# Head norms of a differential attention: given priority on VectorE, and head 7's spreading products one step later on TensorE

## The chip, the cores and the metric

The kernel runs on one core of a Trainium2 chip. The metric is the device time of one execution in microseconds; the time before is the median of three runs. Names of engines: PE is TensorE (PEld its weight loads), DVE is VectorE, ACT is ScalarE, SP is the engine that issues the DMAs.

## The reference

Two post-norm layers over 512 tokens of width 1024. In each layer three branches (a bidirectional state-space scan, a differential attention, a cross-attention to 256 memory tokens) work on projections of x; each branch's output is projected to 1024, weighted by a sigmoid gate, and the sum is projected once more. The change lies in the differential attention, of 8 heads:

```python
q = _apply_rope(dq.reshape(Bsz, S, DIFF_HEADS, 2, DIFF_HEAD_DIM), cos, sin)
k = _apply_rope(dk.reshape(Bsz, S, DIFF_HEADS, 2, DIFF_HEAD_DIM), cos, sin)
v = dv.reshape(Bsz, S, DIFF_HEADS, 2 * DIFF_HEAD_DIM)
o = _diff_attention(q, k, v, lam)          # (softmax_1 - lam * softmax_2) v, per head
o = _rmsnorm(o, diff_norm_w[layer]) * (1.0 - lambda_init)
y_diff = o.reshape(Bsz, S, DIFF_WIDTH) * jax.nn.silu(dg.astype(jnp.float32))
...
merged = (gates[:, :, 0] * jnp.einsum('bse,ed->bsd', y_ssd, w_br_ssd[layer])
          + gates[:, :, 1] * jnp.einsum('bse,ed->bsd', y_diff, w_br_diff[layer])
          + ...)
```

The norm of a head needs 1 / sqrt(mean(o^2) + eps) for each token: one number per token and head, by which 128 channels are multiplied.

## The kernel before, in words

All wide products are done in three passes of split fp32 numbers: a weight `wr` of 512 KB is fetched by SP (line 138), rounded to `wh` by ACT and reduced to the remainder `wl` by DVE (`split`), and each 128-column block is multiplied as wl by xh, wh by xl, wh by xh (`mm3`). The results stand in three PSUM banks `pj`. One such product for 512 tokens is a unit of 24 matmuls. `wr` has two buffers, `wh` and `wl` three each. The engines take their instructions in order. A scheduler sets the order of each, by priorities and estimated times; inside `manual_schedule` PE's own instructions keep the order in which they are written, though others may be put between them. `late(n)` lowers the priority of what is recorded under it by n; `late(-300)` raises it.

The attention of a layer (`diff`) is a list of 35 steps. Each step runs one unit of projection in two halves of 12 matmuls, and puts jobs of the attention before it (`first`) and between its halves (`amid`): `scores` of the next block of 128 queries, `turn` (the transposition of the weights of this one, through the single PSUM bank `pt`, then split into `wT`), `values` for two blocks, and `sums`, which adds up the squares of a head's output (`fth`, held in the tile `sq`) into `ss`. Attention has 32 blocks, steps 0 to 31 (`nst` is 32). The units of steps 28 to 34 are the gates 1 to 7 of this branch; so gate 6 is step 33 and gate 7 step 34.

`norm` (lines 919 to 929) computes the reciprocal norms: a reciprocal, a few products and a Newton iteration (`rsqrt`, tiles rs_q, rs_u, rs_y) in seventeen small instructions on DVE. For heads 0 to 6 `norms` does this in step 30 for 28 columns, transposes the result on PE into `pt` (line 111), copies it to `rt` (ACT), and writes it to DRAM as `rd`. `fin(h)` then reads one row of `rd` back, spread over 128 partitions, into a buffer `fth` (line 954; two buffers, which the squares use too), multiplies the head's output `sdy` with it on DVE, and splits the product into `dy` (rounded half on ACT, remainder on DVE). For head 7 `last` spreads the norms without DRAM: PE multiplies them, broadcast, with the identity into a bank `pm` (pm<-rs_y), and `fin(7)` multiplies with that bank. `last` stands between the halves of step 33.

Behind the steps come the eight branch outputs (`branch_out`): each is a unit of 24 matmuls pj<-dy over the eight heads in order, whose first needs the `dy` of head 0 and whose last that of head 7.

Of the kernel before, what the change touches and what calls it, by code (L numbers as in the profile page):

```python
# [15 lines left out]
ALU = mybir.AluOpType  # L16
# [4 lines left out]
P = 128  # L21
S = 512
D = 1024
KC = D // P
NL = 2
M = 256
EPS = 1e-5
# [14 lines left out]

LX, LD = 70, 80

FILL = (0, 2, 0, 2, 0, 4, 0, 0)

# [3 lines left out]
def bc(ap, shape):  # L52
    return ap.broadcast_to(shape)


class Net:
# [728 lines left out]
    def diff(self, l):  # L785
        nc = self.nc
# [131 lines left out]

        def norm(lo, hi):

            n = 4 * (hi - lo)
            s0, ss = self.s0[:, 4 * lo:4 * hi], self.ss[:, 4 * lo:4 * hi]
            nc.vector.reciprocal(out=s0, in_=s0)
            self.stt(ss, ss, 1.0 / 128.0, s0, ALU.mult, ALU.mult)
            self.tt(ss, ss, s0, ALU.mult)
            self.ts(ss, ss, EPS, ALU.add)
            r = self.rsqrt(self.fp, ss, n)
            self.tt(r, r, s0, ALU.mult)
            return r

        def norms():

            n = 4 * (KC - 1)
            r = norm(0, KC - 1)
            pt = self.bank(self.pt, "pt")
            self.tr(pt[:n, :P], r)
            rt = self.t(self.fp, [n, P], "rt", bufs=1)
            self.act(rt, pt[:n, :P])
            self.rd = self.t(self.dp, [n, P], "rd")
            nc.sync.dma_start(out=self.rd, in_=rt)  # L940

        def last():

            r = norm(KC - 1, KC)
            self.rb = self.bank(self.pm, "pm")
            for c in range(4):
                self.mm(self.rb[:, c * P:(c + 1) * P], bc(r[:, c:c + 1], [P, P]), self.ident)
# [12 lines left out]
        def step(unit, *parts):  # L960

            def f(wh, wl):
                g = fn(wh, wl)
                for p in parts:
                    for job in p:
                        job()
                    next(g, None)
            fn, u = unit
            self.T(f, u)

        def job(fn, *a):
            return lambda: fn(*a)
# [17 lines left out]
        nst = 4 * KC  # L990
        for s, unit in enumerate(units):
            first = [job(scores, s + 1)] if s + 1 < nst else []
            amid = []
            if s % 4 == 2 and s < nst:
                amid.append(job(values, s // 4, 0))
            if s % 4 == 0 and 0 < s <= nst:
                amid.append(job(values, s // 4 - 1, 1))
            if s < nst:
                amid.append(job(turn, s))
            if s % 4 == 1 and 1 < s <= nst + 1:  # L1000
                first.append(job(sums, s // 4 - 1))
            if s == nst - 2:
                amid.append(norms)
            if s == nst + 1:
                amid.append(last)
            step(unit, first, amid)
            if s >= nst - 1:
                for h in range(2 * (s - nst + 1), min(2 * (s - nst + 1) + 2, KC)):
                    self.T(job(fin, h))
        self.T(order.close)  # L1010
        mgs = ([], [])

# [216 lines left out]
```

## Time and profile before

| | us |
|---|---|
| median of 3 runs | 2241.68 (2237.81 to 2244.03) |
| the profiled execution, its own time | 2240.25 |
| its span | 2238.5 |
| PE busy | 2173.2 (97%) |
| DVE busy | 1589.9 (71%) |
| ACT busy | 1004.6 (45%) |
| mean granted PE clock | 0.994 |

The page gives busy times, the chain of work that ended last, and groups of instructions by line. The views of the trace give single instructions with start and length in us from the span's start (the timeline), who waited for whom, and busy times and clock in chosen stretches (windows). In brackets behind an instruction stands how long its engine had been idle before it and whose end released it. The two layers run the same code; attention ends at about 1025 us in the first and 2141 us in the second.

### The profile page before, as it was taken

How to read it: one execution, taken by the hardware profiler on the slowest of the kernel's cores; microseconds unless marked ns; L12 is line 12 of the kernel's file. 1: busy time of each engine (PE TensorE's matmuls, PEld its weight loads, DVE VectorE, ACT ScalarE, POOL GpSimd, SP SyncE). 2: the span in 40 equal slices, each digit the busy share in tenths (PEclk: the TensorE clock that was granted, in tenths of full speed). 3: DMA queues.
4: the chain of work that ended last, by engine and by line, in shares of the span. 5: the costliest groups of instructions: out<-in, count | busy, mean ns of one | idle time of the engine just before them, and what ended most of it. 6: DMA issues, size and time to landing. Idle time of an engine off the chain costs nothing.

```text
span 2238.5 us, 30344 instructions
## 1 busy us (share of the span) xinstructions
PE 2173.2 (97%) x11714; PEld 1787.8 (80%) x11714; DVE 1589.9 (71%) x2468; ACT 1004.6 (45%) x1895; POOL 52.9 (2%) x38
## 2 busy tenths in 40 slices
PE   8999999999999999998999999999999999999898
PEld 6777877788888788877996777787788887888678
DVE  7887888758544777765567888888744547777657
ACT  5664545424432555442355564554423325544430
POOL 0000000000000000000000000010100000000000
PEclk9999999999999999999999999999999999999999
DMA  4654444425453222233564545453433332223333
GB/s 148 180 160 144 147 142 138 126 85 190 145 179 115 90 81 82 81 104 108 163 225 115 165 141 151 132 152 122 123 124 118 116 106 85 78 84 90 109 99 128
DMA packets 108278, 283.79 MB, mean 127 GB/s; under 512 B 12588, under 2 KB 17252, under 8 KB 107876
## 3 DMA queue, kind: packets, MB, share of 16 engines
q1 hardware_dynamic: 108132, 281.84, 41.2%
q8 instruction: 92, 1.51, 0.3%
q14 instruction: 54, 0.44, 0.1%
HBM read 255.55 MB, written 17.85 MB: 122 GB/s over the span
## 4 chain that ended last, share of the span: by engine, by line
PE 71%; DVE 14%; DMA 7%; ACT 5%; issue 2%; SPq 0%; POOL 0%; DVEq 0%; POOLq 0%; ACTq 0%
PE pj L103 59%; PE pm L103 9%; DMA ab<-dab 4%; DVE wl L81 2%; PE pt L111 2%; DVE ab L81 2%; DVE acc L84 2%; ACT ab L91 1%; ACT wh L91 1%; DVE y L81 1%; DVE rx L81 1%; PE pt L103 1%; DMA wr<-wu 1%; DMA fth<-rd 1%; DVE yl L84 1%
## 5 line engine op out<-in xcount | busy, mean ns | idle before, releaser
L103 PE MATMUL pj<-xh,wl 128*128 128x512 f32 x1664 | 669.1, 402 | 10.8 <-DVE wl L81 8.9
L103 PE MATMUL pj<-xh,wh 128*128 128x512 f32 x1664 | 660.8, 397 | 0.0
L103 PE MATMUL pj<-xl,wh 128*128 128x512 f32 x1664 | 658.1, 395 | 0.0
L81 DVE TENSOR_TENSOR wl<-wr,wh 128x1024 fp32r<-128x1024 f32 x330 | 404.5, 1226 | 108.3 <-ACT wh L91 107.5
L91 ACT ACTIVATE wh<-wr 128x1024 fp32r<-128x1024 f32 x330 | 347.4, 1053 | 235.3 <-PE pj L103 199.5
L103 PEld LDWEIGHTS pj<-xh,wl 128*128 128x128 f32 x1664 | 314.1, 189 | 90.8 <-issue 18.3
L103 PEld LDWEIGHTS pj<-xh,wh 128*128 128x128 f32 x1664 | 313.7, 189 | 71.6 <-issue 6.0
L103 PEld LDWEIGHTS pj<-xl,wh 128*128 128x128 f32 x1664 | 314.1, 189 | 63.5 <-issue 3.6
L91 ACT ACTIVATE ab<-ab,bias 128x128 f32<-128x128 f32 x512 | 160.7, 391 | 121.9 <-DVE ab L81 121.3
L84 DVE SCALAR_TENSOR_TENSOR acc<-pj,hcw,acc 128x510 f32<-128x510 f32 x192 | 142.4, 743 | 23.8 <-ACT acc L91 22.4
L91 ACT ACTIVATE fpp<-pm,fmx 128x512 f32<-128x512 f32 x128 | 87.9, 687 | 83.4 <-DVE fmx L881 82.6
L881 DVE TENSOR_REDUCE fmx<-pm 128x1 f32<-128x512 f32 x128 | 87.0, 686 | 45.4 <-PE pm L103 45.1
L103 PE MATMUL pj<-yl,wh 128*128 128x512 f32 x256 | 102.3, 400 | 0.8 <-DVE yl L84 0.8
L103 PE MATMUL pj<-yh,wh 128*128 128x512 f32 x256 | 103.1, 403 | 0.0
L81 DVE TENSOR_TENSOR ab<-ab,cst 128x1024 f32<-128x1024 f32 x64 | 86.3, 1349 | 22.9 <-DMA ab<-dab 22.8
L103 PE MATMUL pj<-dy,wh 128*128 128x512 f32 (+1 forms) x384 | 101.9, 354 | 0.0
L103 PE MATMUL pj<-yh,wl 128*128 128x512 f32 x256 | 101.9, 399 | 0.0
L103 PE MATMUL pj<-cy,wh 128*128 128x512 f32 x256 | 78.8, 389 | 0.0
L103 PEld LDWEIGHTS pj<-dy,wh 128*128 128x128 f32 x384 | 68.0, 189 | 10.0
L103 PE MATMUL pj<-wh,xl 128*128 128x256 f32 x256 | 74.8, 292 | 0.0
L103 PE MATMUL pj<-wl,xh 128*128 128x256 f32 x256 | 72.4, 283 | 0.0
L103 PE MATMUL pj<-wh,xh 128*128 128x256 f32 x256 | 72.3, 283 | 0.0
(273 smaller groups left out, 3387.3 us busy)
## 6 DMA issues: line engine op xcount, KB each, us to landing
wr<-wu SPq DMA_DIRECT2D x336, 512.0 KB, 3.6
ab<-dab SPq DMA_DIRECT2D x64, 512.0 KB, 5.7
eb<-deb SPq DMA_DIRECT2D x64, 256.0 KB, 4.8
mkv<-dkv SPq DMA_DIRECT2D x16, 512.0 KB, 4.3
rsw<-rx SPq DMA_DIRECT2D x128, 64.0 KB, 2.0
dgt<-tg SPq DMA_DIRECT2D x18, 256.0 KB, 2.6
dkv<-mo SPq DMA_DIRECT2D x16, 256.0 KB, 4.0
dkv<-q SPq DMA_DIRECT2D x16, 256.0 KB, 3.7
```

The costliest lines, as they stand in the source:

```text
L81: (eng or self.nc.vector).tensor_tensor(out=out, in0=a, in1=b, op=op)
L84: self.nc.vector.scalar_tensor_tensor(out=out, in0=a, scalar=s, in1=b, op0=op0, op1=op1)
L91: self.nc.scalar.activation(out=out, in_=a, func=f, **kw)
L103: self.nc.tensor.matmul(out=out, lhsT=a, rhs=b, start=first, stop=last)
L111: self.nc.tensor.transpose(out=out, in_=x, identity=self.ident)
L881: nc.vector.tensor_reduce(out=mx[:, c:c + 1], in_=ps, axis=AX.X, op=ALU.min)
```

## The change

`norm` is no longer called by the jobs that use its result. It is recorded by itself, behind step 29 (heads 0 to 6) and behind step 33 (head 7), with its priority on DVE raised by 300. `spread` (before: `norms`) transposes, copies and writes as before, in step 30. `last` moves from step 33 to step 34. The `fin` jobs follow later: heads 0 and 1 behind step 32 (before: 31), heads 2 to 4 behind step 33 (before: 2 and 3 behind 32, 4 and 5 behind 33), heads 5 to 7 behind step 34.

```diff
-LX, LD = 70, 80
+LX, LD, LN = 70, 80, 300
...
         def norm(lo, hi):
-            n = 4 * (hi - lo)
             s0, ss = self.s0[:, 4 * lo:4 * hi], self.ss[:, 4 * lo:4 * hi]
-            nc.vector.reciprocal(out=s0, in_=s0)
-            self.stt(ss, ss, 1.0 / 128.0, s0, ALU.mult, ALU.mult)
-            self.tt(ss, ss, s0, ALU.mult)
-            self.ts(ss, ss, EPS, ALU.add)
-            r = self.rsqrt(self.fp, ss, n)
-            self.tt(r, r, s0, ALU.mult)
-            return r
-
-        def norms():
+            with self.late(-LN):
+                nc.vector.reciprocal(out=s0, in_=s0)
+                self.stt(ss, ss, 1.0 / 128.0, s0, ALU.mult, ALU.mult)
+                self.tt(ss, ss, s0, ALU.mult)
+                self.ts(ss, ss, EPS, ALU.add)
+                self.r = self.rsqrt(self.fp, ss, 4 * (hi - lo))
+                self.tt(self.r, self.r, s0, ALU.mult)
+
+        def spread():
             n = 4 * (KC - 1)
-            r = norm(0, KC - 1)
             pt = self.bank(self.pt, "pt")
-            self.tr(pt[:n, :P], r)
+            self.tr(pt[:n, :P], self.r)
...
         def last():
-            r = norm(KC - 1, KC)
+            r = self.r
...
             if s == nst - 2:
-                amid.append(norms)
-            if s == nst + 1:
+                amid.append(spread)
+            if s == nst + 2:
                 amid.append(last)
             step(unit, first, amid)
-            if s >= nst - 1:
-                for h in range(2 * (s - nst + 1), min(2 * (s - nst + 1) + 2, KC)):
-                    self.T(job(fin, h))
+            if s in (nst - 3, nst + 1):
+                self.T(job(norm, *((0, KC - 1) if s < nst else (KC - 1, KC))))
+            for h in {nst: (0, 1), nst + 1: (2, 3, 4), nst + 2: (5, 6, 7)}.get(s, ()):
+                self.T(job(fin, h))
```

What this makes of the order of the instructions, in the first layer (the second is alike). First PE, from the sums of head 7's squares (pt<-fth) to the first branch output. Before, pj_8870 is gate 6, pj_8938 gate 7, pj_8982 branch output 0, and pm<-rs_y is `last`:

```order
L103 MATMUL pt_8864<-cst_81,fth_8831 128x1 x4
L103 MATMUL pj_8870<-xh_82,wl_8753 128x512
...
L103 MATMUL pm_8903<-cst_81,rs_y_8887 128x128 x4
L103 MATMUL pj_8870<-xh_82,wl_8753 128x512
...
L103 MATMUL pj_8938<-xh_82,wl_8803 128x512
...
L103 MATMUL pj_8982<-dy_1008_6051,wl_8861 128x512
```

In the changed kernel pj_8860 is gate 6, pj_8928 gate 7 and pj_8982 again branch output 0:

```order
L103 MATMUL pt_8854<-cst_81,fth_8821 128x1 x4
L103 MATMUL pj_8860<-xh_82,wl_8753 128x512
...
L103 MATMUL pj_8928<-xh_82,wl_8793 128x512
...
L103 MATMUL pj_8982<-dy_1008_6051,wl_8851 128x512
...
L103 MATMUL pm_8941<-cst_81,rs_y_8891 128x128 x4
L103 MATMUL pj_8928<-xh_82,wl_8793 128x512
...
L103 MATMUL pj_8982<-dy_1009_6052,wh_8850 128x512
```

`last` moved behind the second half of gate 6, the first half of gate 7 (12 matmuls each) and the first ten matmuls of branch output 0, which the scheduler put ahead of it: three for each of the heads 0 to 2 and one for head 3. The second half of gate 7 and the rest of branch output 0 stand behind it. The transposition of the other heads' norms stands where it stood, behind the turn of step 30.

Next DVE, at the end of head 7's norms. The names fth_ are the spread rows that `fin` reads (before: 8927 is head 5, 8965 head 6), wl_ the weights' remainders, dy1 the remainders of the heads, pm_8903 `last`. Before:

```order
L81 TENSOR_TENSOR sdy_1014_6064<-sdy_1014_6064,fth_1526_8927 128x512
L84 SCALAR_TENSOR_TENSOR rs_y_1520_8887<-rs_q_1522_8889,rs_y_1520_8887 128x4
L81 TENSOR_TENSOR rs_q_1522_8889<-rs_y_1520_8887 128x4
L81 TENSOR_TENSOR sdy_1014_6064<-sdy_1014_6064,fth_1532_8965 128x512
L81 TENSOR_TENSOR rs_q_1522_8889<-rs_q_1522_8889,rs_u_1521_8888 128x4
L81 TENSOR_TENSOR dy1_1009_6052<-sdy_1014_6064,dy0_1008_6051 128x512
L84 SCALAR_TENSOR_TENSOR rs_y_1520_8887<-rs_q_1522_8889,rs_y_1520_8887 128x4
L81 TENSOR_TENSOR dy1_1009_6052<-sdy_1014_6064,dy0_1008_6051 128x512
L81 TENSOR_TENSOR rs_y_1520_8887<-rs_y_1520_8887,fs0_1015_6065 128x4
L81 TENSOR_TENSOR sdy_1014_6064<-sdy_1014_6064,pm_1523_8903 128x512
```

In the changed kernel fth_8912 is head 3, 8917 head 4, 8960 head 5, and wl_8925 the weight of branch output 1:

```order
L81 TENSOR_TENSOR sdy_1014_6064<-sdy_1014_6064,fth_1523_8912 128x512
L81 TENSOR_TENSOR rs_q_1521_8893<-rs_y_1519_8891 128x4
L81 TENSOR_TENSOR wl_1527_8925<-wr_1525_8922,wh_1526_8924 128x1024
L81 TENSOR_TENSOR rs_q_1521_8893<-rs_q_1521_8893,rs_u_1520_8892 128x4
L81 TENSOR_TENSOR dy1_1009_6052<-sdy_1014_6064,dy0_1008_6051 128x512
L84 SCALAR_TENSOR_TENSOR rs_y_1519_8891<-rs_q_1521_8893,rs_y_1519_8891 128x4
L81 TENSOR_TENSOR sdy_1014_6064<-sdy_1014_6064,fth_1524_8917 128x512
L81 TENSOR_TENSOR rs_y_1519_8891<-rs_y_1519_8891,fs0_1015_6065 128x4
L81 TENSOR_TENSOR sdy_1014_6064<-sdy_1014_6064,fth_1531_8960 128x512
L81 TENSOR_TENSOR dy1_1009_6052<-sdy_1014_6064,dy0_1008_6051 128x512
L81 TENSOR_TENSOR sdy_1014_6064<-sdy_1014_6064,pm_1529_8941 128x512
```

The norms of head 7 now end between the products of heads 4 and 5, where they ended behind the product of head 6; the product of head 7 comes ahead of that of head 6.

Last SP's queue from the writing of `rd` on. Before:

```order
L940 DMA rd_1497_8734<-rt_1496_8732 28x128
L954 DMA fth_1505_8790<-rd_1497_8734 128x512
L954 DMA fth_1506_8795<-rd_1497_8734 128x512
L138 DMA wr_1515_8858<-wu 128x1024
L138 DMA wr_1527_8932<-wu 128x1024
L954 DMA fth_1513_8848<-rd_1497_8734 128x512
L954 DMA fth_1514_8853<-rd_1497_8734 128x512
L954 DMA fth_1525_8922<-rd_1497_8734 128x512
L138 DMA wr_1534_8976<-wu 128x1024
L954 DMA fth_1526_8927<-rd_1497_8734 128x512
L954 DMA fth_1532_8965<-rd_1497_8734 128x512
```

In the changed kernel:

```order
L938 DMA rd_1497_8734<-rt_1496_8732 28x128
L138 DMA wr_1513_8848<-wu 128x1024
L138 DMA wr_1525_8922<-wu 128x1024
L952 DMA fth_1511_8838<-rd_1497_8734 128x512
L952 DMA fth_1512_8843<-rd_1497_8734 128x512
L952 DMA fth_1522_8907<-rd_1497_8734 128x512
L138 DMA wr_1534_8976<-wu 128x1024
L952 DMA fth_1523_8912<-rd_1497_8734 128x512
L952 DMA fth_1524_8917<-rd_1497_8734 128x512
L952 DMA fth_1531_8960<-rd_1497_8734 128x512
L138 DMA wr_1540_9013<-wu 128x1024
L952 DMA fth_1532_8965<-rd_1497_8734 128x512
```

The reads for heads 0 and 1 moved behind two weight loads. Heads 0, 1, 2 take the places of heads 2, 3, 4, heads 3 and 4 those of 5 and 6, and the reads for heads 5 and 6 follow, the last behind one more weight load.

## The prediction

> **What bounds the kernel now.** I read the page's busy times and its chain first.
>
> ```profile
> PE 2173.2 (97%) x11714; PEld 1787.8 (80%) x11714; DVE 1589.9 (71%) x2468; ACT 1004.6 (45%) x1895; POOL 52.9 (2%) x38
> PE 71%; DVE 14%; DMA 7%; ACT 5%; issue 2%; SPq 0%; POOL 0%; DVEq 0%; POOLq 0%; ACTq 0%
> ```
>
> TensorE (PE) sets the end, so an edit is worth what it takes from PE's idle or slow time. The view of waits, for PE alone, in the stretch where attention ends, shows two waits in the first layer (the second layer's long one is in the timeline below). Columns: waiting and awaited group, total us, times, longest.
>
> ```profile
> PE pm L103 <- DVE rs_y L81: 8.2, 1, 8.2
> PE pt L111 <- DVE wT L81: 1.4, 1, 1.4
> ```
>
> The long one is `last`: the spreading products (pm<-rs_y) stand between the halves of gate 6 and wait for head 7's norms. The timeline of PE (start, length; 30 products from 1018.14 to 1024.95), first layer and second:
>
> ```profile
> 1005.44 0.39 PE L103 MATMUL pj<-xh,wh 128*128 128x512 f32 x1
> 1013.99 2.08 PE L103 MATMUL pm<-cst,rs_y 128*128 128x128 f32 x8 [8.16 <-DVE rs_y L81]
> 1018.14 0.39 PE L103 MATMUL pj<-xh,wl 128*128 128x512 f32 x1
> 1024.95 0.39 PE L103 MATMUL pj<-dy,wl 128*128 128x512 f32 x1
> 2121.04 0.39 PE L103 MATMUL pj<-xh,wh 128*128 128x512 f32 x1
> 2129.38 2.08 PE L103 MATMUL pm<-cst,rs_y 128*128 128x128 f32 x8 [7.96 <-DVE rs_y L81]
> 2140.74 0.39 PE L103 MATMUL pj<-dy,wl 128*128 128x512 f32 x1
> ```
>
> A product of 512 columns takes 6.81 / 30 = 0.227 us. PE could have gone on at 1005.44 + 0.23 = 1005.67, but started its first branch product (pj<-dy) at 1024.95: 19.28 us, for `last` and 36 products. What `last` costs when PE isn't cold stands in the branch before, where the same eight matmuls spread another norm:
>
> ```profile
> 455.42 1.13 PE L103 MATMUL pm<-cst,rs_y 128*128 128x128 f32 x8
> 456.31 0.48 PE L103 MATMUL pj<-yh,wh 128*128 128x512 f32 x1
> 456.62 0.40 PE L103 MATMUL pj<-yh,wl 128*128 128x512 f32 x1
> ```
>
> That is 0.89, and 0.08 more for the first product behind it: 0.97. So 0.97 + 36 x 0.227 = 9.14 us would do, and the wait costs 10.1 us in the first layer (10.3 in the second, from 2121.27 to 2140.74): 8.3 idle, and 1.8 (2.2) because PE comes back slow. The windows (PE, PEld, DVE, ACT, POOL busy, granted clock, DMA share, GB/s) show that:
>
> ```profile
> 1014.00:1018.50 4.50, 4.50 (x16) 3.98 (x17) 1.38 (x2) 0.63 (x1) 0.00 (x0) 0.58 0.00 0
> 1018.50:1025.00 6.50, 6.50 (x31) 5.37 (x30) 1.23 (x1) 1.64 (x2) 0.00 (x0) 1.00 0.21 56
> ```
>
> The clock is 0.58 just after the wait and 1.00 later. [...]
>
> From there to the layer's end the chain is PE alone (start, length), so what is won stays won:
>
> ```profile
> 1016.06 120.43 PE pj L103 x804
> 2131.46 97.78 PE pj L103 x612
> ```
>
> **The change part by part.** No instruction is added or removed; rows move.
>
> *The first seven heads' norms go ahead on DVE.* Their transposition does not move on PE. It waits today for its PSUM bank (wT evicts it), not for the norms:
>
> ```profile
> 976.13 0.75 DVE L84 SCALAR_TENSOR_TENSOR fpp<-fpp,fsm 128x512 f32<-128x512 f32 x1
> 979.22 0.19 DVE L81 TENSOR_TENSOR rs_y<-rs_y,fs 128x28 f32<-128x28 f32 x1
> 984.31 0.60 PE L111 MATMUL pt<-cst,fpp 128*128 128x128 f32 x4
> 986.32 0.28 PE L111 MATMUL pt<-cst,rs_y 128*28 128x128 f32 x1 [1.41 <-DVE wT L81]
> ```
>
> The norms were done at 979.4, 6.9 us before that. So this part gains nothing. It costs nothing either: fpp, which is pushed back by the small norm instructions (at most a dozen, 0.2 us each), has from 976.9 to 984.3. Without that cover it would be 2.4 us a layer.
>
> *`last` moves behind 24 gate products and 10 branch products on PE.* That is cover for the wait: 34 x 0.227 = 7.7 us, so PE reaches `last` at 1013.39 instead of 1005.67. What it then finds depends on two things, both worked out for the first layer by putting the new orders onto the times that the old slots show.
>
> *The heads' rows come later.* On SP's queue the first two reads fth<-rd, the row that spreads a head's norms, now stand behind two more weight loads. Heads 0, 1, 2 take the slots that heads 2, 3, 4 had. The queue's timeline, and the landing times of fth<-rd:
>
> ```profile
> 988.30 0.82 SPq L954 DMA_DIRECT2D fth<-rd  x2
> 998.62 0.42 SPq L954 DMA_DIRECT2D fth<-rd  x1
> 1003.03 0.80 SPq L954 DMA_DIRECT2D fth<-rd  x2
> 1007.16 0.99 SPq L954 DMA_DIRECT2D fth<-rd  x2
> DMA to landing us min/median/max: 3.1/3.7/3.9
> ```
>
> and DVE's products with them:
>
> ```profile
> 1002.32 0.69 DVE L81 TENSOR_TENSOR sdy<-sdy,fth 128x512 f32<-128x512 f32 x1 [1.46 <-DMA fth<-rd]
> 1003.88 1.23 DVE L81 TENSOR_TENSOR wl<-wr,wh 128x1024 fp32r<-128x1024 f32 x1 [0.87 <-ACT wh L91]
> 1006.44 0.69 DVE L81 TENSOR_TENSOR sdy<-sdy,fth 128x512 f32<-128x512 f32 x1 [0.74 <-DMA fth<-rd]
> 1007.12 0.69 DVE L81 TENSOR_TENSOR sdy<-sdy,fth 128x512 f32<-128x512 f32 x1
> 1009.51 0.16 DVE L81 TENSOR_TENSOR rs_q<-rs_y 128x4 f32<-128x4 f32 x1
> 1009.71 0.16 DVE L81 TENSOR_TENSOR rs_q<-rs_q,rs_u 128x4 f32<-128x4 f32 x1
> 1010.91 0.69 DVE L81 TENSOR_TENSOR sdy<-sdy,fth 128x512 f32<-128x512 f32 x1 [0.45 <-DMA fth<-rd]
> 1013.78 0.15 DVE L81 TENSOR_TENSOR rs_y<-rs_y,fs 128x4 f32<-128x4 f32 x1
> ```
>
> Heads 0 to 3 are multiplied at 1002.3, 1006.4, 1007.1 and 1010.9. There are two fth buffers, so head 4's row is read when head 2's product ends (1007.8), head 5's after head 3's (1011.6), head 6's after head 4's.
>
> *Head 7's norms.* In DVE's new order head 3's product (1010.91 to 1011.6) is followed by a weight remainder wl (1.23, to 1012.8), head 3's remainder dy (0.69, to 1013.5) and head 4's product (to 1014.2) before the last rs_y: 1014.25. That is 0.3 us later than its 1013.93 now. So "ahead on DVE" doesn't bring head 7's norms forward; they still hang on the landings that DVE waits for in between. PE has the ten branch products' data in time (heads 0 to 2 are split by 1009.4; head 3's first half, on ACT, by 1012.3, and is wanted at 1013.16). PE waits 0.9 us at `last`. A gap of 1.4 us, the transposition's, shows what such a gap does to the clock:
>
> ```profile
> 986.68 0.39 PE L103 MATMUL pj<-xl,wh 128*128 128x512 f32 x1
> 986.91 0.40 PE L103 MATMUL pj<-xh,wh 128*128 128x512 f32 x1
> ```
>
> The pitch behind it is 0.23 at once, so I count no slow clock.
> *The rest of branch output 0.* A head's halves take (min/median/max, ns)
>
> ```profile
> L91 ACT ACTIVATE dy<-sdy x16: 617/630/631, 993.0 to 2132.2; 128x512 fp32r<-128x512 f32 x16
> L81 DVE TENSOR_TENSOR dy<-sdy,dy x16: 681/686/693, 994.0 to 2132.9; 128x512 fp32r<-128x512 f32 x16
> ```
>
> `last` ends at 1014.31 + 0.97 = 1015.28, gate 7's second half at 1018.00, eight products for heads 3 to 5 at 1019.8. Head 5's row lands at 1011.65 + 3.7 = 1015.35; head 6's is issued at 1014.25 and lands at 1017.95. DVE does head 5's product (to 1016.0), head 4's remainder (1016.65), head 7's product (1017.25), the remainders of 5 and 7 (1018.65), head 6's product (1019.3). ACT then halves head 6 (0.63, to 1020.0, behind gate 7's tanh), DVE takes its remainder by 1020.7. PE wants that at 1020.05: 0.9 us of waiting in all from 1019.8. With five products more, branch output 0 is done at 1021.9. Today it is done at 1024.95 + 24 x 0.227 = 1030.4.
>
> **Sum.** First layer 8.5 us. In the second layer the slots lie 1115.6 us later almost exactly (2121.27 against 1005.67), and its old excess is 0.2 larger: 8.7. Together 17.2. The profiled execution took 2240.25 us with a span of 2238.5, so its successor would have a span of 2221.3 and take 2223.1; against the median of the runs, 2241.68, which is 1.4 above it, 2224.5. That is the forecast. A measurement of this kernel can tell about 0.3%, 6.7 us, from no change.
>
> Bounds: at best PE waits for nothing, 10.1 + 10.3 = 20.4 us, 2221.3. At worst for the same mechanism the landings are all 3.9 and each step on DVE or ACT that I packed tightly slips a little, 2 us a layer: 2228.5.
>
> **Rivals.**
>
> *Head 7's norms come so late that the clock drops again.* By the rows the gap that does it lies between 1.4 us (it didn't) and 8.0 (it did); I take 4, nearer to the first, as an estimate. Then rs_y slips by 3.1 us. For it: DVE works in order, and three awaited things (a row, a weight, a row) stand ahead of rs_y. Against: each has a slot in the trace, with at most 1.5 us of waiting. Price: 3.1 + 2.0 for the clock, less the 0.9 at head 6 that it then covers: 4.2 a layer, 2232.9. [...]
>
> *Everything hides* (head 6's row and rs_y a microsecond earlier each): 2221.3.
>
> *Slower: the two fth buffers become the bound.* Branch products now stand ahead of `last` and of half of gate 7, and their data starts ten microseconds later (998.62 against 988.30). One buffer carries heads 0, 2, 4, 6 in turn, four trips. The gain is gone when head 6 is 8.5 us later than I have it: 2.1 us a trip, a landing of 5.8 instead of 3.7. At 7.0 it is 13.2 - 8.5 = 4.7 us lost a layer: 2251. The slowest row of the kind is
>
> ```profile
> ab<-dab SPq DMA_DIRECT2D x64, 512.0 KB, 5.7
> ```
>
> with twice the bytes, and the fth rows lie between 3.1 and 3.9 with weight loads beside them. So it is unlikely.
>
> *Nothing moves*: since rs_y isn't done earlier than today, the wait could simply stay if PE's new rows waited for their data as long as PE waited for rs_y. With a landing of 5.7 that is so: 4 x 2.0 = 8 of the 8.5, 2240.7.
>
> **How the numbers follow.** Forecast 0.78; all hidden 0.08; clock drop 0.08; nothing 0.04; slower 0.02. The forecast, all hidden and the drop are faster by over 0.3%: 0.94. The range goes from 2219 (all hidden, 2 us for the scatter of the runs, 2237.8 to 2244.0) to 2233 (the clock drop).
>
> **What would show it.** In the profile after: PE's wait at `last` under 2 us, with DVE's rs_y ending about where it did; PE's branch products beginning before `last`, at about 1011.1; a short wait of dy before the end of branch output 0; the granted clock near 1.00 through 1005 to 1025; fth<-rd first issued at about 998.6, still landing in 3 to 4 us. I am wrong if the wait turns up at pj<-dy for several microseconds, if rs_y ends after 1016, or if the clock still falls.

## The result, and the profile after

| | before | after |
|---|---|---|
| median of the runs (us) | 2242.53 (6 runs, 2237.81 to 2244.36) | 2222.06 (6 runs, 2220.18 to 2229.46) |
| the profiled execution (us) | 2240.25 | 2229.46 |
| its span (us) | 2238.5 | 2227.7 |
| mean granted PE clock | 0.994 | 0.995 |

The ratio is 0.9914, with an interval of 0.9897 to 0.993: the change takes 20.5 us by the medians, and between 16 and 23 by the interval. The profiled execution happens to be the longest of the six; the other five lie between 2220.18 and 2222.32. What made it long stands in the last section.

The page's busy times and chain hardly differ from those before, since no instruction was added or removed:

```profile
PE 2176.8 (98%) x11714; PEld 1789.9 (80%) x11714; DVE 1588.1 (71%) x2468; ACT 1004.9 (45%) x1895; POOL 53.9 (2%) x38
PE 70%; DVE 14%; DMA 8%; ACT 6%; issue 2%; SPq 0%; POOL 0%; POOLq 0%; DVEq 0%; ACTq 0%
```

The change shows in the waits. PE's own, at the end of attention in the first layer and then in the second:

```profile
PE pt L111 <- DVE wT L81: 1.4, 1, 1.4
PE pm L103 <- DVE rs_y L81: 0.7, 1, 0.7
...
PE pm L103 <- DVE rs_y L81: 1.3, 1, 1.3
```

The wait at `last` fell from 8.2 and 8.0 us to 0.7 and 1.3. The transposition's wait of 1.4 stayed, as its place did.

The timeline of PE in both layers: the sums of head 7 (pt<-cst,fth), the first branch product, `last`, and in the first layer the first product behind `last` (1016.47), the last two of head 6 (1021.51) and the first product of branch output 1 (1022.77):

```profile
1003.30 0.95 PE L103 MATMUL pt<-cst,fth 128*128 128x1 f32 x8
1012.40 0.39 PE L103 MATMUL pj<-dy,wl 128*128 128x512 f32 x1
1015.56 1.16 PE L103 MATMUL pm<-cst,rs_y 128*128 128x128 f32 x8 [0.73 <-DVE rs_y L81]
1016.47 0.48 PE L103 MATMUL pj<-xh,wl 128*128 128x512 f32 x1
1021.51 0.73 PE L103 MATMUL pj<-dy,wh 128*128 128x512 f32 x2
1022.77 0.39 PE L103 MATMUL pj<-dy,wl 128*128 128x512 f32 x1
2115.33 0.95 PE L103 MATMUL pt<-cst,fth 128*128 128x1 f32 x8
2124.43 0.39 PE L103 MATMUL pj<-dy,wl 128*128 128x512 f32 x1
2128.14 1.16 PE L103 MATMUL pm<-cst,rs_y 128*128 128x128 f32 x8 [1.28 <-DVE rs_y L81]
```

The branch products begin before `last`. The eight matmuls of `last` take 1.16 on the row, close to the 1.13 of the undisturbed spreading in the branch before, not 2.08; PE does not come back slow. The windows (PE, PEld, DVE, ACT, POOL busy, granted clock, DMA share, GB/s) say the same: the clock is 1.00 on both sides of `last`, where it was 0.58 behind it before.

```profile
1010.00:1015.00 5.00, 4.83 (x22) 3.67 (x20) 4.20 (x14) 2.15 (x3) 0.00 (x0) 1.00 0.42 139
1015.00:1020.00 5.00, 4.44 (x23) 3.82 (x24) 4.29 (x8) 2.37 (x4) 0.00 (x0) 1.00 0.52 171
```

DVE's timeline: the product of head 3, a weight's remainder, the products of heads 4 and 5 with the last rs_y between them, and the last remainder that branch output 0 wants, head 6's:

```profile
1012.18 0.69 DVE L81 TENSOR_TENSOR sdy<-sdy,fth 128x512 f32<-128x512 f32 x1 [0.64 <-DMA fth<-rd]
1012.86 1.22 DVE L81 TENSOR_TENSOR wl<-wr,wh 128x1024 fp32r<-128x1024 f32 x1
1014.75 0.68 DVE L81 TENSOR_TENSOR sdy<-sdy,fth 128x512 f32<-128x512 f32 x1
1015.35 0.16 DVE L81 TENSOR_TENSOR rs_y<-rs_y,fs 128x4 f32<-128x4 f32 x1
1015.96 0.69 DVE L81 TENSOR_TENSOR sdy<-sdy,fth 128x512 f32<-128x512 f32 x1 [0.46 <-DMA fth<-rd]
1020.76 0.69 DVE L81 TENSOR_TENSOR dy<-sdy,dy 128x512 fp32r<-128x512 f32 x1 [0.91 <-ACT dy L91]
```

This execution reaches the sums 1.29 us later than the one before (1003.30 against 1002.01); all times here are to be read less 1.29. Then rs_y ends at 1014.22, where the forecast had 1014.25.

SP's queue, and the landing of the rows:

```profile
999.90 5.21 SPq L952 DMA_DIRECT2D fth<-rd  x3
1008.42 4.79 SPq L952 DMA_DIRECT2D fth<-rd  x3
1015.46 0.32 SPq L952 DMA_DIRECT2D fth<-rd  x1
DMA to landing us min/median/max: 3.0/3.5/4.3
```

From the sums of head 7 to the first product of branch output 1 the first layer took 1030.38 - 1002.01 = 28.4 us before (the start of branch output 1 is the first branch product's, 1024.95, and 24 x 0.227 behind it) and takes 1022.77 - 1003.30 = 19.5 now; the second took 28.6 and takes 20.0. That is 8.9 + 8.6 = 17.5 us. By this measure all profiled executions can be set side by side. The first number runs from the span's start to the sums in the first layer, the second to its branch output 1, the third to the sums in the second layer, the fourth to its branch output 1, the last to the end:

| us | to sums | attention's end 1 | between | attention's end 2 | to the end |
|---|---|---|---|---|---|
| before | 1002.0 | 28.4 | 1087.2 | 28.6 | 92.3 |
| after | 1003.3 | 19.5 | 1092.6 | 20.0 | 92.4 |
| after, again | 1000.1 | 20.4 | 1087.2 | 19.6 | 92.3 |
| priority alone | 1001.3 | 29.3 | 1088.1 | 28.6 | 92.3 |
| `last` later alone | 1000.8 | 19.7 | 1086.1 | 19.8 | 92.3 |
| reads later alone | 1001.4 | 28.9 | 1089.3 | 29.6 | 92.3 |
| wait filled | 1000.3 | 26.7 | 1087.4 | 27.1 | 92.4 |
| no priority | 1001.0 | 19.7 | 1084.9 | 19.9 | 92.3 |
| no priority, again | 1001.7 | 20.8 | 1087.4 | 20.0 | 92.3 |
| transposition later | 998.3 | 20.5 | 1091.2 | 19.8 | 92.3 |
| `last` and transposition | 999.2 | 19.8 | 1087.9 | 20.9 | 92.3 |
| three buffers | 999.1 | 19.1 | 1085.3 | 19.2 | 92.3 |

In the last column nothing differs. The long stretch between scatters by 8 us, in code that the edits don't touch, except for the transposition's 1.4 us a layer, which counts to the first and third columns. The profiled execution of after lost its 5.4 us there; what makes up the scatter stands in the last section.

### The profile page after: what moved, and what is told of

Same layout as the page of the kernel before. It is cut to its first block, busy times and chain, and to the rows that moved or that the text cites. A ratio compares the mean times of both kernels' runs of the same rounds, so it can differ in the third digit from the quotient of the medians.

```text
span 2227.7 us, 30345 instructions
## 1 busy us (share of the span) xinstructions
PE 2176.8 (98%) x11714; PEld 1789.9 (80%) x11714; DVE 1588.1 (71%) x2468; ACT 1004.9 (45%) x1895; POOL 53.9 (2%) x38
## 4 chain that ended last, share of the span: by engine, by line
PE 70%; DVE 14%; DMA 8%; ACT 6%; issue 2%; SPq 0%; POOL 0%; POOLq 0%; DVEq 0%; ACTq 0%
PE pj L103 58%; PE pm L103 9%; DMA ab<-dab 4%; DVE wl L81 3%; PE pt L111 2%; DVE ab L81 2%; DVE acc L84 2%; ACT ab L91 1%; ACT wh L91 1%; DMA wr<-wu 1%; DVE rx L81 1%; DVE y L81 1%; DMA fth<-rd 1%; PE pt L103 1%; DVE yl L84 1%
## 5 line engine op out<-in xcount | busy, mean ns | idle before, releaser
L103 PEld LDWEIGHTS pj<-xh,wl 128*128 128x128 f32 x1664 | 314.6, 189 | 90.4 <-issue 18.5
L81 POOL TENSOR_TENSOR sqa<-sqa,sz 128x512 f32<-128x512 f32 x32 | 52.7, 1646 | 852.4 <-ACT sz L91 852.4
```

What stands on the lines that cost most here:

```text
L81: (eng or self.nc.vector).tensor_tensor(out=out, in0=a, in1=b, op=op)
L103: self.nc.tensor.matmul(out=out, lhsT=a, rhs=b, start=first, stop=last)
```

## The experiments

Times are medians; ratios are to the kernel before on the same chip, with their 95% intervals. Before took 2241.90 us beside the first four, 2241.92 beside the next four, and 2241.55 beside the two that were run again.

### The priority alone

```diff
-            nc.vector.reciprocal(out=s0, in_=s0)
-            ...
-            r = self.rsqrt(self.fp, ss, n)
-            self.tt(r, r, s0, ALU.mult)
+            with self.late(-300):
+                nc.vector.reciprocal(out=s0, in_=s0)
+                ...
+                r = self.rsqrt(self.fp, ss, n)
+                self.tt(r, r, s0, ALU.mult)
```

> Only the raised priority of the norms; last stays between the halves of gate 6 and the heads' reads stay where they were. My theory (the gain comes from where the spreading products stand on PE, since head 7's norms hang on the landings of the heads' rows): rs_y still ends about 8 us after PE arrives, so the time is that of before within 2 us, about 2242, and PE still waits 8 us at pm<-rs_y in each layer. The rival (the priority brings the norms forward): PE's wait falls below 4 us and the time by 8 us or more, below 2235.

2241.94 us, 1.0 (0.999 to 1.0009). The wait at `last`, first layer:

```profile
PE pm L103 <- DVE rs_y L81: 8.1, 1, 8.1
```

As long as before. The norms' instructions were not held back by their priority: raised, they end no earlier, and rs_y comes 11.9 us behind the sums in both kernels.

### `last` one step later alone

In the kernel before, `last` calls `norm` itself, so head 7's norms are recorded a step later too.

```diff
-            if s == nst + 1:
+            if s == nst + 2:
                 amid.append(last)
```

> Only last is moved from step 33 to step 34, its norms with it and without priority; the heads' reads stay early. The order puts 24 gate products and 12 branch products ahead of pm<-rs_y. My theory: PE arrives 8.2 us later, rs_y ends at about the same place, heads 0 to 3 are ready long before, so the wait shrinks to about half a microsecond and the clock stays at 1.00: 18 to 20 us less than before, 2222 to 2225, the whole gain of the change. The rival (priority and the later reads are needed too): less than half of it, above 2233.

2220.72 us, 0.9914 (0.99 to 0.9927), the ratio of the whole change. PE's wait, first layer and second:

```profile
PE pm L103 <- DVE rs_y L81: 1.2, 1, 1.2
...
PE pm L103 <- DVE rs_y L81: 1.3, 1, 1.3
```

This one line gives the result. The waits are longer than the 0.5 that was expected: rs_y comes 13.2 us behind the sums here and 12.2 in after; this pair does not tell whether the priority or the later reads bring that microsecond. It buys nothing, since the two layers' ends come out within 0.3 us of after's.

### The reads later alone

```diff
-            if s >= nst - 1:
-                for h in range(2 * (s - nst + 1), min(2 * (s - nst + 1) + 2, KC)):
-                    self.T(job(fin, h))
+            for h in {nst: (0, 1), nst + 1: (2, 3, 4), nst + 2: (5, 6, 7)}.get(s, ()):
+                self.T(job(fin, h))
```

> Only the heads' reads and products are recorded later, as in the change; last and the norms as before. My theory: DVE still waits for a landing (1010.9) ahead of rs_y, so PE still waits about 8 us and comes back slow: 2242 within 2 us. The rival (the heads' work in front of head 7's norms on DVE is what held rs_y up, so that recording it later frees them): rs_y some 4 us earlier and the time 8 us or more below that of before.

2240.55 us, 0.9993 (0.9985 to 1.0002).

```profile
PE pm L103 <- DVE rs_y L81: 8.1, 1, 8.1
```

The waits stayed at 8.1 and 8.3. The reads' place neither helps nor harms by itself.

### The wait filled with products that nobody uses

Before, with 34 matmuls of 512 columns ahead of `last`; their results are not read.

```diff
+            for i in range(34):
+                self.mm(self.rb, self.xh[:, i % 8, :P], self.xl[:, i % 8, :])
```

> The kernel before, with 34 products of 512 columns ahead of last into the bank that last then overwrites: they are not used, and they keep PE busy for 7.7 of the 8 us that it waits. If the slow clock after the wait is a price of its own (my theory: 1.8 and 2.2 us in the two layers), the time falls by about 4 us, to 2238.5, though work was added, and the window behind the wait shows a granted clock of 1.00. If the slow products behind the wait have another cause, or the clock falls anyway, nothing is gained, 2242 or more.

2237.55 us, 0.9981 (0.9971 to 0.9992). The timeline of PE: the 34 products, `last`, the first branch product; and the window behind `last`:

```profile
1003.92 7.87 PE L103 MATMUL pm<-xl,xh 128*128 128x512 f32 x34
1012.26 1.16 PE L103 MATMUL pm<-cst,rs_y 128*128 128x128 f32 x8 [0.47 <-DVE rs_y L81]
1021.48 0.39 PE L103 MATMUL pj<-dy,wl 128*128 128x512 f32 x1
```

```profile
1012.00:1016.50 4.50, 4.24 (x23) 3.64 (x24) 1.58 (x4) 0.90 (x2) 0.00 (x0) 1.00 0.00 0
```

`last` stands where it stood, 12.0 us behind the sums, and PE does 7.7 us of useless work; yet the kernel is 4.4 us faster. From the start of `last` to the first branch product it takes 1021.48 - 1012.26 = 9.22 us, against the 9.14 worked out without the slow clock. The six gaps in the traces of before, of the priority alone and of the reads alone took 10.96, 11.36, 11.91, 11.38, 11.46 and 12.08 for the same, 11.53 in the mean. One of them, of the priority alone:

```profile
1013.27 2.08 PE L103 MATMUL pm<-cst,rs_y 128*128 128x128 f32 x8 [8.11 <-DVE rs_y L81]
1025.18 0.39 PE L103 MATMUL pj<-dy,wl 128*128 128x512 f32 x1
```

So the slow clock is a price of its own: 2.4 us a gap in the mean, and it changes from gap to gap (1.8 to 2.9), though the idle time ahead is 8.0 to 8.3 in all six. The clock itself says the same: over the 6.8 us from the start of `last` its mean was 0.72, 0.66, 0.57, 0.65, 0.64 and 0.55 in the six, which is 1.9 to 3.1 us of lost clock, each within 0.2 of that gap's price.

### The change without the priority, twice

```diff
-LX, LD, LN = 70, 80, 300
+LX, LD, LN = 70, 80, 0
```

> The change with the raised priority taken away (LN is 0). The scheduler then puts 19 branch products, up to head 6, ahead of pm<-rs_y instead of 10, and rs_y stands behind head 5's product on DVE. My theory: PE waits at pj<-dy for heads 4 and 6 and gate 7's second half comes later; branch output 0 ends about 2.3 us later a layer than in the change: 4 to 5 us slower than the change, 2226 to 2228. A rival (priority is worth nothing): as the change, 2222. Another (the priority is what gains): near the kernel before, above 2235.

2219.64 us, 0.9897 (0.9883 to 0.9912): the expected loss is not there. The norms do come later, as was expected: rs_y ends at 1015.71 by DVE's timeline, 14.7 us behind the sums (12.2 in after).

```profile
1015.55 0.15 DVE L81 TENSOR_TENSOR rs_y<-rs_y,fs 128x4 f32<-128x4 f32 x1
```

But the scheduler answered: it put 19 branch products ahead of `last` instead of ten. PE's timeline shows some of these products waiting a little for the later heads' data, and `last` for nothing:

```profile
1013.40 0.72 PE L103 MATMUL pj<-dy,wl 128*128 128x512 f32 x2 [0.44 <-ACT dy L91]
1014.90 0.73 PE L103 MATMUL pj<-dy,wh 128*128 128x512 f32 x2 [0.30 <-DVE dy L81]
1015.76 1.16 PE L103 MATMUL pm<-cst,rs_y 128*128 128x128 f32 x8
```

Nine more products are 2.0 us of cover, and by the starts of PE's rows the two waits cost 1.3 us, 0.7 of it idle. So PE reaches `last` 3.3 us later than in after, where it then waited 0.7 us, and rs_y is only 2.5 us later: the wait has moved to the branch products. My error was to take a wait on DVE for a wait on PE without looking at what the scheduler puts in between. By the two medians the priority would even cost 2.4 us, but they come from separate comparisons; so both kernels ran once more on one chip.

> The changed kernel with the raised priority set to 0 once more, on the same chip as the changed kernel beside it. Theory: the place of last makes the gain alone and the priority is worth nothing, because the products that the scheduler puts ahead of last cover the later norms; the two medians lie within 1.5 us and their intervals overlap. Rival: the priority costs 2.4 us, as the two medians of different chips (2222.06 and 2219.64) would say; then this one is lower by 2 us or more.

> The changed kernel as it is, once more. In its first profile the stretch from branch output 1 of the first layer to the sums of head 7 in the second took 1092.6 us against 1087.2 in before, with the same code. Theory: that is scatter between executions (where the clock happens to drop in the scan), not the change; another profiled execution has 1085 to 1089 there most likely, and the attention's end, from head 7's sums to branch output 1, has 19.3 to 20.2 us a layer again. Rival: the change itself brings the drops; then the stretch has 1091 or more again. Median expected 2221 us.

The changed kernel took 2222.88 us, 0.9915 (0.9901 to 0.9928), and without priority 2223.32, 0.9911 (0.9897 to 0.9926). The priority is worth nothing that can be measured, in either direction. The profiles are as close, though in the new one without priority the branch products wait longer in the first layer (1.3 and 0.5 us): the layers' ends take 20.8 and 20.0 us, against 20.4 and 19.6. In the new profile of after the stretch between the layers' ends takes 1087.2 us, as in before: the 1092.6 of the first profile were its own.

### The transposition behind the next half unit

In the changed kernel the transposition of the other heads' norms still stands where it stood, with its wait of 1.4 us. Here it moves from the middle of step 30 to the start of step 31, behind twelve products:

```diff
-            if s == nst - 2:
-                amid.append(spread)
+            if s == nst - 1:
+                first.append(spread)
```

> The change with the transposition of the other heads' norms moved to the start of step 31, where its PSUM bank has long been read; it stands there 12 products later on PE. My theory: the 1.4 us wait of pt<-rs_y goes in both layers and nothing takes its place, since the reads of the heads' rows stand behind weight loads anyway: 2.8 us less than the change, about 2219.3. The rival: the heads' rows come later by the same time and PE waits for dy instead: as the change, 2222.

2220.22 us, 0.9896 (0.9879 to 0.9913). The waits of PE, first layer, have no line for pt<-wT any more, but two for the branch products' data:

```profile
PE pm L103 <- DVE rs_y L81: 0.7, 1, 0.7
PE pj L103 <- ACT dy L91: 0.5, 1, 0.5
PE pj L103 <- DVE dy L81: 0.2, 1, 0.2
```

The 1.4 us are gone in both layers. The two lines for the branch products are no price of that: the changed kernel's second profile has the same two, 0.5 and 0.2, with the transposition in its old place. In the time the gain can't be told. The change itself has 0.9914 and 0.9915, on other chips, and its intervals overlap with this one; on the same chip the kernel without priority, with the transposition in its old place, has 0.9897.

### `last` and the transposition, without the rest

Before, with `last` in step 34 and the transposition ahead of step 31; the norms stay in step 30. Not shown: `norms` is split into the norms and `spread`.

```diff
+            if s == nst - 1:
+                first.append(spread)
-            if s == nst + 1:
+            if s == nst + 2:
                 amid.append(last)
```

> The kernel before with last moved to step 34 (as in the run with that alone) and the transposition moved to the start of step 31, no priority, reads early. My theory: both gains add, 20 + 2.8 us less than before: about 2219. The rival: the transposition's later place delays the early reads and head 7's norms with them, and PE waits at last again: 2222 or more.

2219.84 us, 0.9897 (0.9881 to 0.9913). PE's wait at `last` in the second layer grew:

```profile
PE pm L103 <- DVE rs_y L81: 2.3, 1, 2.3
```

Two edits of place, without priority and without later reads, give no less than the whole change. Whether the transposition adds to `last` alone (0.9914) can't be told here either, since the intervals overlap.

### Three buffers for the rows

The kernel with the later transposition, and three fth buffers for two; to make room, rs_y, rs_u and rs_q have one. Shown is the line for the rows; the two others that make a fth buffer change alike:

```diff
-                rb = self.t(self.fp, [P, S], "fth")
+                rb = self.t(self.fp, [P, S], "fth", bufs=3)
```

> As the run with the transposition at the start of step 31, and three fth buffers instead of two (the norms' small tiles get one buffer instead of two to make room). The order then has 17 branch products ahead of pm<-rs_y. If the two buffers hold back the heads (in the change head 6's remainder came 0.4 us late and rs_y 0.7 to 1.3 us late), the rest of PE's waits goes: 2 us less than that run, about 2217. If rs_y is then held up by more work in front of it on DVE, the wait at last grows instead and the time is 2220 or more.

2216.67 us, 0.9881 (0.9866 to 0.9896). Its four executions (2212.75 to 2217.18) all lie below the four of the same kernel with two buffers (2217.25 to 2223.88), and it is the fastest of all here, about 25 us below before. PE waits, in the first layer, for one thing alone:

```profile
PE pm L103 <- DVE rs_y L81: 0.6, 1, 0.6
```

The layers' ends take 19.1 and 19.2 us, 2.0 less together than with two buffers; the waits for the heads' data that are gone, 0.7 in the first layer and 0.2 in the second, are half of it. The scheduler's order differs too: it has 17 branch products ahead of `last` for ten, so the buffers and the order are not told apart. The rest of the 3.5 us between the medians lies in stretches that scatter by more; whether the third buffer, which the squares use too, has a part in it is open.

## Why the prediction was right

**What bounds the kernel.** The wait at `last` and the slow clock behind it were the thing. `last` alone in its later place has the ratio of the whole change, and the other two edits alone do nothing.

**The size.** Forecast 8.5 + 8.7 = 17.2 us; the two ends of attention in the profiles give 17.5, and 16.9 with the second profile of after; the medians give 20.5 and, measured again, 18.7. The forecast lies inside both intervals. That it meets 17.5 within 0.3 us is in part luck, since the second profile's first layer ends 1.0 us later than the first's. Part of what the medians have above it fits the slow clock: I charged it by the one profile at 1.8 and 2.2, where six gaps have 2.4 in the mean, 0.8 us more for both layers. The rest I put down to the scatter of the stretch between; that is not shown.

**`last` and head 7's norms.** Less the 1.29 us, PE was to reach `last` at 1013.39 and reached it at 1013.54; rs_y was to end at 1014.25 and ended at 1014.22. The wait was forecast at 0.9 and was 0.7, in the second layer 1.3. The reason given holds: "ahead on DVE" did not bring head 7's norms forward against the old time, since in DVE's order an awaited row, a weight's remainder and two more instructions stand ahead of the last rs_y. What I could not see from before is that the priority does bring them forward against the same kernel without it, by 2.5 us in the first pair of profiles and 3.7 in the second (first layer), and that the scheduler's filling makes this worthless.

**The rest of branch output 0.** It was to be done at 1021.9, and was at 1021.5 (1022.77 less 1.29). The step that was too dear is head 6: its product began at 1017.9 (DVE's 1019.16 less 1.29) for 1018.6, and the wait was 0.4 instead of 0.9, as the weight loads of PE show:

```profile
PEld pj L103 <- DVE dy L81: 0.4, 1, 0.4
```

In the first layer of the second profile of after it was 0.8 (0.54 and 0.22, on PE's own rows), so the two sizes are within what executions differ by.

**The transposition.** Forecast: it stays where it is with its 1.4 us. So it did.

**The rivals.** The clock did not drop at the gaps of 0.7 and 1.3 us at `last` (1.00 in the windows behind both), nor at the 2.3 of `last` and transposition, where it was 1.00 in the window behind the wait and the pitch of the products 0.23 us. But the 4 us at which that rival let the clock fall, an estimate between 1.4 and 8.0, was too long: elsewhere in these traces the clock fell behind waits of 2.0 to 2.9 us (last section). So the rival was nearer than its estimate of 4 us says, and that the clock held behind the 2.3 was partly luck. The two fth buffers did not become the bound: rows landed in 3.0 to 4.3 us. They may cost something: the kernel with three has ends 1 us shorter a layer, with another order as well. This lies in the direction of that rival, at about an eighth of the 8.5 us at which it would have decided.

## What to carry to other kernels

PE took its instructions in order here: in the kernel before, `last` waited 8.2 us in the first layer and 8.0 in the second, and 34 products that run ahead of it in the changed kernel stood behind it. Move the waiting instruction behind work that is ready, and count that work against the time at which the awaited result was ready before; raising the priority of the awaited work brought it no earlier in one order here and 2.5 us earlier in another, and bought no time in either. The six gaps of 8.0 to 8.3 us on PE cost 1.8 to 2.9 us each more than their length, so even useless products in them paid: 4.4 us. And where a scheduler fills the place, look at what it put there before charging a later result to PE.

## What the runs showed of the hardware

Two things may surprise. First, the clock drops in the state-space scan too, behind waits of about 2 to 3 us, in some executions and not in others. Windows of 50 us, in before, then in the first profile of after, then in the second; where only two are shown, the other two up to 1350 us read 1.00:

```profile
1150.00:1200.00 50.00, 47.43 (x267) 38.80 (x266) 34.55 (x50) 25.65 (x39) 0.52 (x1) 1.00 0.49 162
1200.00:1250.00 50.00, 45.61 (x216) 34.52 (x215) 38.89 (x62) 26.64 (x54) 0.00 (x0) 0.97 0.51 133
```

```profile
1150.00:1200.00 50.00, 46.29 (x229) 37.10 (x229) 35.05 (x52) 23.09 (x35) 0.53 (x1) 0.97 0.39 115
1200.00:1250.00 50.00, 46.89 (x221) 35.64 (x220) 39.19 (x59) 27.74 (x62) 2.51 (x1) 0.97 0.57 152
1250.00:1300.00 50.00, 46.87 (x252) 38.20 (x250) 46.49 (x60) 30.42 (x67) 5.23 (x4) 0.97 0.64 182
1300.00:1350.00 50.00, 47.90 (x204) 36.50 (x203) 37.09 (x49) 26.17 (x58) 0.00 (x0) 0.97 0.37 106
```

```profile
1150.00:1200.00 50.00, 48.31 (x243) 39.05 (x244) 37.28 (x57) 23.42 (x35) 0.13 (x1) 1.00 0.40 122
1200.00:1250.00 50.00, 45.44 (x214) 34.87 (x214) 38.76 (x55) 26.58 (x60) 1.52 (x1) 0.93 0.63 159
```

A granted clock of 0.97 over 50 us is 1.5 us of lost clock; a single drop comes to 1.7 us (0.75 over the 6.8 us behind the waits at 1220.44, 1282.86 and 1329.72 in the first profile of after), in two cases in the scan to 3.1 (0.54). In the first profile of after there are four, each behind one of its four longest waits there, 2.1 to 2.9 us:

```profile
1282.86 1.69 PE L103 MATMUL pm<-m,xsT 128*64 128x128 f32 x16 [2.16 <-DVE m L81]
```

In the second run without priority a wait of 2.20 us (at 1217.73) left the clock at 1.00. Over all twelve traces, from 150 us on, the clock of the 6.8 us behind a wait of PE fell below 1.00 for none of 48 waits from 1.3 to 1.97 us, 12 of 23 from 1.98 to 2.51, all eight from 2.57 to 2.87 and all six of about 8. A shorter wait can be enough too: one of 1.2 us ahead of eight one-column products (pt<-sqa, about 1.05 us), the same twice in every trace, was followed by a drop in 12 of 24 cases (0.75 behind the one at 452.08 in the first profile of after, 1.00 behind the one at 451.83 in before).

These drops and the waits make up the scatter of the stretch between. Before lost 1.7 us of clock there, with PE idle for 18.5 us; the first profile of after 6.8 and 19.8; the second 5.2 and 16.0. Less both, the stretch lasts 1065.6 to 1067.0 us in all twelve traces. So the 5.4 us of the first profile are lost clock in the main against before, but longer waits in the main against the second profile. Why the waits differ is open.

By these counts the length of a wait does not decide alone: of the waits of 1.98 to 2.51 us about half were followed by a drop, and the price behind the six of 8.0 to 8.3 us went from 1.8 to 2.9. What else counts the runs don't settle.

Second, work that is of no use made the kernel faster by 4.4 us, since 7.7 us of products in a wait of 8 kept the clock at 1.00 (window 1012.00 to 1016.50) where it was 0.58 before (1014.00 to 1018.50).
